# Five of the projections of a two-layer trunk by seven block products instead of eight

## The chip, the cores and the metric
One core of a Trainium2 chip runs the whole program. The metric is device time in microseconds (us) of one execution. TensorE (PE) multiplies; VectorE (DVE), ScalarE (ACT) and GpSimd (POOL) work on tiles in SBUF; SyncE (SP) issues nearly all DMAs. TensorE writes to PSUM, from which the other engines read.

## The reference
Two layers on 2048 + 256 tokens of width 1024, in float32. Layer A is attention in a window, layer B a bidirectional mLSTM; each norms its input, gates its output and adds it to x.

```python
def window_attention_mixer(xn, w_in, sink, w_out):
    proj = xn @ w_in
    q, k, v, z = jnp.split(proj, ...)          # 1024, 256, 256, 1024 columns
    ...                                        # rope, softmax over a band of keys, with a sink
    return (o * jax.nn.silu(z)) @ w_out

def mlstm_mixer(xn, w_in, gate_bias, head_norm, w_out):
    proj = xn @ w_in
    q, k, v, o, z, g = jnp.split(proj, cuts, axis=-1)   # 512, 512, 1024, 1024, 1024, 16 columns
    ...                                        # forward and backward mLSTM in chunks, summed, normed by head
    h = h * jax.nn.sigmoid(o) * jax.nn.silu(z)
    return h @ w_out

def trunk(x, ...):
    for i in range(DEPTH):
        xn = rms_norm(x, norm_g[i])
        x = x + (window_attention_mixer(xn, ...) if i % 2 == 0 else mlstm_mixer(xn, ...))
    return rms_norm(x, final_norm_g)
```

## The kernel before
The 2304 tokens are 18 tiles of 128. A product in float32 is made of three matmuls in a faster 32-bit format: `split` and `load_w` cut each operand into a rounded part "hi" (a cast, mostly on ScalarE) and a rest "lo" (a subtraction, mostly on VectorE), and `project` adds hi*hi, hi*lo and lo*hi in PSUM (L166 to L168). A projection of one tile to one block of 512 columns is 8 K tiles of 128 times these three, 24 matmuls with the activations as weights of the array (128x128) and the weight matrix as the moving 128x512 operand.

The stages follow each other: `attn_core` (q, k, v and the attention, a software pipeline of generators over the tiles), `attn_out` (z gate, times the attention's output O^T read back from DRAM, out projection, residual, norm, and the transposed xn2T written to DRAM), `mlstm_qkv` (five column blocks of a tile), `gate_sums`, `mlstm_gates_states` (the o and z gates, four blocks of a tile, and the backward states between them), `mlstm_core`. Weights lie as hi/lo slots in SBUF: 16 in the pool `w`, 8 in `wy`, 8 in `wx`, so that the blocks of the next stage can be formed while the last is still in use. Raw pieces stream through small rings (`rawx` 3, `raww` 4, split activations `xhi`/`xlo` 4).

The order within each engine is not written out by hand: a list scheduler places the instructions of the whole program by their dependences, buffers and its own estimates, and each engine then works through its own list in that order. An instruction whose input is late holds up all that stand behind it on its engine.

Of the kernel before, what the change touches and what calls it, by code (L numbers as in the profile page):

```python
# [35 lines left out]
NXB = 0  # L36
# [8 lines left out]
PH1, PL1 = (1, 5), (4,)  # L45
LASTB = (0, 1, 2, 3)
EA, ES, EQ = 2, 18, 0
ORDER = "cubwbubccucbcbuwubbbbbbw"
PHI = (1, 3, 5, 7)
PLO = (2, 6)  # L50
# [9 lines left out]
class Trunk:  # L60
    def __init__(self, nc, tc, ctx, a):
# [10 lines left out]
        # the gates of all tokens and what follows from them; layer A's staging of O^T before  # L72
# [6 lines left out]
        # reciprocal softmax sums, in the attention output's order of heads  # L79
        self.den = cp.tile([128, NT, 2, 4, 2], F32, tag="den", name="den")  # L80
        self.wp = ctx.enter_context(tc.tile_pool(name="w", bufs=16))
        self.sp = ctx.enter_context(tc.tile_pool(name="stage", bufs=1))
        self.xp = ctx.enter_context(tc.tile_pool(name="xparts", bufs=NXA))
        self.slots = lambda pool, n: [(pool, {"tag": "xhi"}, {"tag": "xlo"})] * n
        self.xring, self.nx = self.slots(self.xp, NXA), 0
# [3 lines left out]
        self.xn2T = dt("xn2T", [128, D])  # L89
# [6 lines left out]
    def stage(self, src, tag="rawx", bufs=None, pool=None):  # L96
        """A streamed [128, n] piece of DRAM."""
        n = src.shape[-1]
        raw = (pool or self.sp).tile([128, UW], F32, tag=tag, name=tag, bufs=bufs or NRX)
        self.nc.sync.dma_start(raw[:, :n], src)  # L100
        return raw[:, :n]

    def split(self, src, eng=None):
        """hi/lo float32r parts of four [128, 128] K tiles."""
        nc = self.nc
        # a ring over the pools' slots
        pool, *kw = self.xring[self.nx % len(self.xring)]
        self.nx += 1
        hi, lo = (pool.tile([128, 512], F32R, name=n, **k) for n, k in zip(("xhi", "xlo"), kw))
        nc.scalar.copy(hi[:], src)  # L110
        (eng or nc.vector).tensor_sub(lo[:], src, hi[:].bitcast(F32))  # L111
# [6 lines left out]
    def load_w(self, src, units, g=None, first=0, pool_hi=(), pool_lo=(), before={}):  # L118
        """All slabs of a weight matrix, column unit by column unit; w[block][kt] = (hi, lo, width)."""
# [3 lines left out]
        for i, widths in enumerate(units, first):  # L123
            n = sum(widths)
            pool = self.wp if i < 2 else (self.wy if i == 2 else self.wx)
            blocks = [[] for _ in widths]
            for kt in range(KT):
                if kt in before:
                    fn, *args = before[kt]
                    fn(*args)  # L130
                uw = UW if i == 3 else 512
                lo = pool.tile([128, uw], F32R, tag="wl", name="wlo")
                hi = pool.tile([128, uw], F32R, tag="wh", name="whi")
                raw = self.stage(src[kt * 128:(kt + 1) * 128, c0:c0 + n], "raww", NRW)
                gk = None if g is None else g[:, kt:kt + 1]
                if kt in pool_lo:
                    if g is not None:
                        nc.gpsimd.tensor_scalar(raw, raw, gk, 1.0, ALU.mult, ALU.mult)
                    nc.scalar.copy(hi[:, :n], raw)
                    nc.gpsimd.tensor_sub(lo[:, :n], raw, hi[:, :n].bitcast(F32))  # L140
                else:
                    if kt in pool_hi:
                        nc.gpsimd.tensor_scalar(hi[:, :n], raw, 1.0 if g is None else gk, 1.0, ALU.mult, ALU.mult)
                    elif g is None:
                        nc.scalar.copy(hi[:, :n], raw)
                    else:
                        nc.scalar.activation(hi[:, :n], raw, AF.Copy, scale=gk)  # L147
                    if g is None:
                        nc.vector.tensor_sub(lo[:, :n], raw, hi[:, :n].bitcast(F32))
                    else:  # L150
                        nc.vector.scalar_tensor_tensor(lo[:, :n], raw, gk, hi[:, :n].bitcast(F32), ALU.mult, ALU.subtract)  # L151
                c = 0
                for j, wd in enumerate(widths):
                    blocks[j].append((hi[:, c:c + wd], lo[:, c:c + wd], wd))
                    c += wd
# [3 lines left out]

    def project(self, o, xs, wb, kts=range(KT)):  # L160
        """o = x @ (one column block of w), in three float32r passes."""
# [8 lines left out]
    def rms(self, pool, src, out, n=D):  # L170
        """out[128,1] = (mean(src^2) + eps)^-1/2"""
# [11 lines left out]
    def attn_core(self):  # L183
        nc, tc, a = self.nc, self.tc, self.a
        with ExitStack() as st:
# [43 lines left out]
            def q(t, hf, xs, cs):  # L229
# [4 lines left out]
                # rotary embedding: y = x * [cos|cos] + swap(x) * [-sin|sin]  # L234
# [7 lines left out]
                # even head of a pair: [hi; lo], odd head: [lo; hi]  # L242
# [9 lines left out]
            # the first tiles' halves come between the first slabs that meet them  # L252
# [4 lines left out]

            w = self.load_w(a["w_qkv"], [[512]], self.g[:, 0], before={k: (half, t, h) for k, t, h in STARTS})
# [6 lines left out]
            w += self.load_w(a["w_qkv"][:, 512:], [[512]] * 2, self.g[:, 0], first=1)  # L265

            def core(t):
# [9 lines left out]
                def scores():  # L277
                    for g in range(KVH):
# [27 lines left out]
                        # the weights stay unnormalised; 1 / sum joins the gate  # L306
# [52 lines left out]
    def attn_out(self):  # L359
        nc, tc, a = self.nc, self.tc, self.a  # L360
        with ExitStack() as st:
            pg = st.enter_context(tc.tile_pool(name="a2g", bufs=4, reuse_waits="tile"))
            p = st.enter_context(tc.tile_pool(name="a2", bufs=2, reuse_waits="tile"))
            pt = st.enter_context(tc.tile_pool(name="a2tr", bufs=1, space=PSUM, reuse_waits="tile"))
            ps = st.enter_context(tc.tile_pool(name="a2ps", bufs=1, space=PSUM, reuse_waits="tile"))
            G = {}

            X, HG = {}, {}

            def load(t):  # L370
                X[t] = self.load_x(a["xT"][t])

            def zgate(t, b):
                pz = self.pj()
                self.project(pz, X[t], wz[b])
                rs = self.rstd[:, t:t + 1]
                gt = pg.tile([128, 512], F32, tag="G", name="G")
                nc.scalar.activation(gt[:], pz[:], AF.Sigmoid, scale=rs)
                nc.vector.scalar_tensor_tensor(gt[:], pz[:], rs, gt[:], ALU.mult, ALU.mult)
                gh = gt[:].rearrange("p (h d) -> p h d", d=HD)  # L380
                nc.gpsimd.tensor_mul(gh, gh, self.den[:, t, b].rearrange("p c g -> p (c g)").unsqueeze(2).to_broadcast([128, 8, HD]))
                G[t, b] = gt

            def gated(t):
                HG[t] = []
                for b in range(2):
                    oT = self.wg.tile([128, 512], F32, tag="oT", name="oT")
                    nc.sync.dma_start(oT[:], self.oT[t][:, b * 512:(b + 1) * 512])
                    tp = pt.tile([128, 4, 128], F32, tag="tr", name="tr")
                    for j in range(4):  # L390
                        nc.tensor.transpose(tp[:, j, :], G[t, b][:, j * 128:(j + 1) * 128], self.ident[:])
                    nc.vector.tensor_mul(oT[:], oT[:], tp[:].rearrange("p c q -> p (c q)"))
                    HG[t] += self.split(oT[:])

            def residual(t):
                x = p.tile([128, D], F32, tag="x", name="x", bufs=2)
                nc.sync.dma_start(x[:], a["x"][t * 128:(t + 1) * 128, :])
                return x

            def out(t, b, x):  # L400
                po = (ps.tile([128, 512], F32, tag="po", name="po", bufs=2) if t else self.pj())
                self.project(po, HG[t], wo[b])
                nc.vector.tensor_add(x[:, b * 512:(b + 1) * 512], x[:, b * 512:(b + 1) * 512], po[:])  # L403

            def norm(t, x):
                nc.sync.dma_start(self.x2[t][:], x[:])
                rs = p.tile([128, 1], F32, tag="rs", name="rs", bufs=2)
                self.rms(p, [x[:, :512], x[:, 512:]], rs[:])
                nc.gpsimd.tensor_scalar(x[:], x[:], rs[:], 1.0, ALU.mult, ALU.mult)
                for b in range(2):  # L410
                    tp = ps.tile([128, 4, 128], F32, tag="tr2", name="tr2", bufs=1)
                    for j in range(4):
                        nc.tensor.transpose(tp[:, j, :], x[:, (b * 4 + j) * 128:(b * 4 + j + 1) * 128], self.ident[:])
                    xo = p.tile([128, 4, 128], F32, tag="xo", name="xo", bufs=2)
                    nc.scalar.copy(xo[:], tp[:])
                    nc.sync.dma_start(self.xn2T[t][:, b * 512:(b + 1) * 512], xo[:].rearrange("p c q -> p (c q)"))

            load(0)
            load(1)
            wz = self.load_w(a["w_z"], [[512]] * 2, self.g[:, 0], 0, PHI, PLO)  # L420
            wo = self.load_w(a["w_ao"], [[512]], None, 2, PHI, PLO)
            for b in range(2):
                for t in range(2):
                    zgate(t, b)
            for t in range(NT):
                if t > 1 and t + 1 < NT:
                    load(t + 1)
# [496 lines left out]
```

## Time and profile before

| what | value |
|---|---|
| runs | 2364.59, 2367.21, 2369.46 us; median 2367.21 |
| profiled execution | span 2366.8 us, mean granted TensorE clock 0.994 |
| TensorE busy | 2323.3 us, 98% |
| VectorE / ScalarE / GpSimd busy | 1122.7 / 904.8 / 392.1 us |
| HBM read / written | 185.01 / 78.41 MB |

The times of the runs and the profiled span are those of whole executions; the profile lists no other time of its own execution than the span. Busy times of TensorE come from records that overlap. A line of the groups names the source line, the engine, the operation, the tiles out<-in, how often it runs, its busy time and mean duration, and the idle time before it with what ended it.

### The profile page before, as it was taken

Reading aid. Unit: us, or ns where it says so; the run is one execution under the profiler, and the core shown is the slowest. Engines: PE = TensorE matmul, PEld = TensorE weight load, DVE = VectorE, ACT = ScalarE, POOL = GpSimd, SP = SyncE. Lnnn points to the kernel's source line nnn. Section 1 sums busy time; section 2 is a strip of 40 time slices with the busy share of each in tenths; the row PEclk is TensorE's granted clock in tenths of the full one; section 3 lists DMA queues with packets and bytes.
Section 4 is the critical chain, followed back from the end, with each engine's and each line's share of the span. In section 5 each row is a group of like instructions: output and inputs, shape, how many; then the busy total and the mean of one; then the engine's idle time right before and its main releaser. Section 6 shows DMA issues by size and latency. Waiting matters only on the chain.

```text
span 2366.8 us, 31795 instructions
## 1 busy us (share of the span) xinstructions
PE 2323.3 (98%) x11582; PEld 1853.7 (78%) x11582; DVE 1122.7 (47%) x2731; ACT 904.8 (38%) x2149; POOL 392.1 (17%) x372
## 2 busy tenths in 40 slices
PE   8999999999999999999999999999999999999998
PEld 6767666767677888887788888888888887888887
DVE  5566656565864222225311111353333336777785
ACT  5454545454564222224211111343222236554453
POOL 3212121211321111113100000000000003333320
PEclk9999999999999999999999999999999999999999
DMA  6211111111214333335422221444323346566651
GB/s 219 65 42 47 42 47 38 52 33 43 94 63 146 119 103 116 107 116 174 139 90 82 75 85 72 147 137 151 104 89 112 104 137 214 190 223 214 211 177 67
DMA packets 129659, 265.49 MB, mean 112 GB/s; under 512 B 14272, under 2 KB 17120, under 8 KB 129504
## 3 DMA queue, kind: packets, MB, share of 16 engines
q1 hardware_dynamic: 129360, 263.46, 33.6%
q8 instruction: 91, 1.49, 0.3%
q14 instruction: 64, 0.52, 0.1%
q10 hardware_dynamic: 144, 0.01, 0.0%
HBM read 185.01 MB, written 78.41 MB: 111 GB/s over the span
## 4 chain that ended last, share of the span: by engine, by line
PE 40%; DMA 3%; DVE 3%; ACT 2%; POOL 2%; issue 1%; SPq 0%; POOLq 0%; DVEq 0%; ACTq 0%
PE pj L166 12%; PE pj L168 12%; PE pj L167 12%; DMA qs<-rows 2%; PE cu L614 1%; DVE hh L764 1%; ACT E L723 1%; POOL qs L728 1%; PE tr L457 1%; DVE xlo L111 1%; PE num L743 1%; POOL ss L757 1%; PE num L745 0%; DMA E<-rows 0%; DVE x L804 0%
## 5 line engine op out<-in xcount | busy, mean ns | idle before, releaser
L166 PE MATMUL pj<-whi,xhi 128*128 128x512 f32 (+2 forms) x2320 | 893.9, 386 | 12.7 <-ACT whi L147 5.8
L168 PE MATMUL pj<-whi,xlo 128*128 128x512 f32 (+2 forms) x2320 | 884.1, 384 | 5.1 <-DVE xlo L111 5.1
L167 PE MATMUL pj<-wlo,xhi 128*128 128x512 f32 (+2 forms) x2320 | 886.1, 382 | 0.0
L168 PEld LDWEIGHTS pj<-whi,xlo 128*128 128x128 f32 x2320 | 438.2, 189 | 100.5 <-issue 13.0
L166 PEld LDWEIGHTS pj<-whi,xhi 128*128 128x128 f32 x2320 | 438.6, 189 | 100.0 <-ACT whi L147 11.7
L167 PEld LDWEIGHTS pj<-wlo,xhi 128*128 128x128 f32 x2320 | 438.3, 189 | 81.1 <-issue 4.9
L302 ACT ACTIVATE Sm<-Sm,nm 128x384 f32<-128x384 f32 (+1 forms) x288 | 166.9, 581 | 69.4 <-DVE nm L296 69.1
L291 DVE CUSTOM_DVE_ANT_0 Sm<-s,mask 128x384 f32<-128x384 f32 (+1 forms) x272 | 137.1, 528 | 80.0 <-PE s L289 76.8
L329 PE MATMUL o<-PT,V 128*64 128x512 f32 x400 | 146.3, 620 | 4.7 <-DVE PT L319 4.7
L110 ACT CAST xhi<-rawx 128x512 fp32r<-128x512 f32 x144 | 87.4, 618 | 156.3 <-PE pj L167 100.8
L316 PEld LDWEIGHTS ptp<-ident,Sm 128*128 128x128 f32 x800 | 93.8, 141 | 62.7 <-issue 33.3
L316 PE MATMUL ptp<-ident,Sm 128*128 128x128 f32 x800 | 125.7, 278 | 2.3 <-ACT PT L319 1.6
L151 DVE SCALAR_TENSOR_TENSOR wlo<-raww,g,whi 128x512 fp32r<-128x512 f32 (+1 forms) x112 | 93.4, 857 | 50.0 <-ACT whi L147 36.6
L319 DVE COPY PT<-ptp 128x512 f32<-128x512 f32 x128 | 86.8, 686 | 62.1 <-PE ptp L316 28.6
L166 PE MATMUL po<-whi,xhi 128*128 128x512 f32 x272 | 108.2, 398 | 1.3 <-DVE x L403 1.3
L167 PE MATMUL po<-wlo,xhi 128*128 128x512 f32 x272 | 107.0, 394 | 0.0
L168 PE MATMUL po<-whi,xlo 128*128 128x512 f32 x272 | 104.3, 393 | 0.0
L176 ACT ACTIVATE junk<-x 128x512 bf16<-128x512 f32 x72 | 45.3, 630 | 151.4 <-DVE x L403 128.6
L111 DVE TENSOR_TENSOR xlo<-rawx,xhi 128x512 fp32r<-128x512 f32 x110 | 75.0, 696 | 58.3 <-ACT xhi L110 56.4
L288 PE MATMUL s<-KH,Q 128*128 128x384 f32 (+1 forms) x288 | 100.9, 362 | 0.9 <-DVE mx L291 0.8
L618 DVE SCALAR_TENSOR_TENSOR C<-C,scr,cu 128x258 f32<-128x258 f32 x112 | 52.3, 477 | 90.4 <-PE cu L614 89.4
L289 PE MATMUL s<-KL,Q 128*128 128x384 f32 (+1 forms) x288 | 92.1, 330 | 0.0
(194 smaller groups left out, 2965.1 us busy)
## 6 DMA issues: line engine op xcount, KB each, us to landing
rawx<-xT SPq DMA_DIRECT2D x72, 256.0 KB, 2.9
x<-x SPq DMA_DIRECT2D x36, 512.0 KB, 2.6
rawx<-xn2T SPq DMA_DIRECT2D x72, 256.0 KB, 3.8
rawx<-v SPq DMA_DIRECT2D x68, 258.0 KB, 3.2
go<-go SPq DMA_DIRECT2D x32, 512.0 KB, 3.6
v<-v SPq DMA_DIRECT2D x18, 516.0 KB, 3.6
rawx<-x SPq DMA_DIRECT2D x36, 256.0 KB, 2.8
oT<-scr SPq DMA_DIRECT2D x36, 256.0 KB, 2.0
```

What stands on the lines that cost most here:

```text
L110: nc.scalar.copy(hi[:], src)
L111: (eng or nc.vector).tensor_sub(lo[:], src, hi[:].bitcast(F32))
L151: nc.vector.scalar_tensor_tensor(lo[:, :n], raw, gk, hi[:, :n].bitcast(F32), ALU.mult, ALU.subtract)
L166: nc.tensor.matmul(o[:, :n], xh, wh, start=kt == 0, stop=False)
L167: nc.tensor.matmul(o[:, :n], xh, wl, start=False, stop=False)
L168: nc.tensor.matmul(o[:, :n], xl, wh, start=False, stop=kt == KT - 1)
L288: nc.tensor.matmul(S[:, :nk, :], q, KH[:, g, win, :], start=True, stop=False)
L289: nc.tensor.matmul(S[:, :nk, :], q, KL[:, g, win, :], start=False, stop=True)
L291: nc.vector.tensor_tensor_reduce(Sm[:, :nk], S[:, :nk], mask[:, t % 3, win, :], 1.0, MASKED, ALU.add, ALU.max, mx[:, c:c + 1])
L302: nc.scalar.activation(Sg[c][:, :nk], Sg[c][:, :nk], AF.Exp, bias=nm[:, c:c + 1], scale=HD ** -0.5, accum_out=rs[:, c:c + 1])
L316: nc.tensor.transpose(tp[:, c, :], Ss[g][c][:, j, :], self.ident[:])
L329: nc.tensor.matmul(o[gg * 64:(gg + 1) * 64, :], vof[sl[j]][:, g * HD:(g + 1) * HD], PTs[g][j][:], start=j == 0, stop=j == nk - 1)
```

## The change
Five projections of 1024 columns (z, out, q|k together, and o|z as two halves) are computed on pairs of tiles: the two tiles' 256 tokens by 1024 features are cut into quarters a11, a12 (first tile's halves), a21, a22 (second tile's), the weight matrix into b11 to b22 of 512x512. Seven products of sums and differences of these quarters (Winograd's form) replace eight products of quarters. `WOPS` and `XOPS` name the operands in the order of use.

```python
XOPS = ("a11", "s2", "a12", "s3", "s1", "a22", "s4")
WOPS = ("b11", "t2", "b21", "t3", "t1", "t4", "b22")

def winograd_w(self, src, c0, g=None):          # 28 hi/lo slots; L196 scales a raw piece by g
    def part(op, i, raw):
        hi, lo = self.slot()
        at[op, i] = self.taken[-1]
        nc.scalar.copy(hi[:], raw)                               # L202
        nc.vector.tensor_sub(lo[:], raw, hi[:].bitcast(F32))     # L203
        W[op][i] = hi[:], lo[:], 512
    for i in range(4):
        part("b11", i, load(i, 0, 0))
    for i in range(4):
        t1, b12, b22, b21 = load(i, 0, 0), load(i, 0, 1), load(i, 1, 1), load(i, 1, 0)
        t2 = self.raw("raww")[:, :512]
        nc.gpsimd.tensor_sub(t1, b12, t1)                        # L211
        nc.gpsimd.tensor_sub(t2, b22, t1)                        # L212
        part("t2", i, t2)
        part("b21", i, b21)
        nc.gpsimd.tensor_sub(b12, b22, b12)                      # L215
        part("t3", i, b12)
        part("t1", i, t1)
        nc.gpsimd.tensor_sub(b21, b21, t2)                       # L218
        part("t4", i, b21)
        part("b22", i, b22)

def winograd_x(self, s0, s1, X):                # seven split() (L124 cast, L125 lo) a pair
    a11 = load(s0, 0);  X["a11"] = self.split(a11);  yield
    a21, a22 = load(s1, 0), load(s1, 1)
    nc.gpsimd.tensor_add(x1, a21, a22)                           # L236
    nc.gpsimd.tensor_sub(x2, x1, a11)                            # L237
    X["s2"] = self.split(x2);  yield
    ...                                         # L243 a11 - a21 for s3, L248 a12 - x2 for s4

def half_product(self, o, xs, ws, more=False):  # 12 matmuls, L258 to L260
    ...

def winograd(self, pair, X, W, use, side):      # side(): the next step of the next pair's winograd_x
    a, b = self.pj(), self.pj()
    self.half_product(a[:], X["a11"], W["b11"])
    nc.scalar.copy(u1, a[:]);                                        side()
    self.half_product(b[:], X["s2"], W["t2"])
    nc.vector.tensor_add(u2, u1, b[:]);                              side()   # L273
    self.half_product(a[:], X["a12"], W["b21"], True)
    use(t0, 0, a[:], None);                                          side()
    self.half_product(c[:], X["s3"], W["t3"])
    nc.vector.tensor_add(u3, u2, c[:]);                              side()   # L280
    self.half_product(d[:], X["s1"], W["t1"])
    use(t1, 1, d[:], u3);                                            side()
    self.half_product(c[:], X["a22"], W["t4"], True)
    use(t1, 0, c[:], u2);                                            side()
    self.half_product(d[:], X["s4"], W["b22"], True)
    use(t0, 1, d[:], u2);                                            side()
```

`use` is what a stage does with a block: it adds u to it (in L525 for z, L559 for out, both VectorE; in L558 GpSimd adds u to x) and goes on as before (sigmoid, G at L529, times den at L531, times O^T at L537). The same diff makes these moves:

- `attn_out` is cut in two passes over all tiles: `attn_gate` writes the gated, transposed tiles to DRAM (`hgT`), and `attn_out` reads them as its activations. The residual comes in halves, and xn2T is multiplied by the row g on VectorE as it leaves PSUM, so that the weights of layer B are no longer scaled.
- `mlstm_qkv` does q|k on pairs of tiles and then v and the gates tile by tile, with xn2T read a second time; `mlstm_gates_states` does the two halves of o|z one after the other, with xn2T read for each, and one backward state after each pair. The o|z products all go to DRAM, and `mlstm_core` reads them back.
- Weights live in 31 hi/lo slots taken from one queue (16 + 8 + `NWX` 7), of which a pass uses 28; the next pass takes the three that are free and then each slot as the last pair is done with it, in the order of `WOPS`.
- The rings grow between the two cores: split activations 4 to 6, `rawx` 3 to 6, `raww` 4 to 7. Two PSUM banks (c, d) come from a pool of their own.

How the lists of the engines change is seen at three places. First TensorE, near the end of the attention core: the scores' transposes (ptp) and O = P V (o) of the last tiles, and the z projection (pj). Before:

```order
L167 MATMUL pj<-wlo,xhi 128x512
L168 MATMUL pj<-whi,xlo 128x512
L166 MATMUL pj<-whi,xhi 128x512 [waits DVE_49]
L316 MATMUL ptp<-ident,Sm 128x128 [waits Activation_49]
L316 MATMUL ptp<-ident,Sm 128x128
L316 MATMUL ptp<-ident,Sm 128x128 [waits Activation_49]
L316 MATMUL ptp<-ident,Sm 128x128
L316 MATMUL ptp<-ident,Sm 128x128 [waits Activation_49]
L316 MATMUL ptp<-ident,Sm 128x128
L167 MATMUL pj<-wlo,xhi 128x512
L316 MATMUL ptp<-ident,Sm 128x128 [waits Activation_49]
L316 MATMUL ptp<-ident,Sm 128x128
```

After, the last P V products and the start of the z pass:

```order
L484 MATMUL o<-PT,V 64x512
L484 MATMUL o<-PT,V 64x512 [waits Activation_49]
L484 MATMUL o<-PT,V 64x512
L484 MATMUL o<-PT,V 64x512 [waits DVE_49]
L258 MATMUL pj<-whi,xhi 128x512 [waits Activation_49]
L259 MATMUL pj<-wlo,xhi 128x512
L260 MATMUL pj<-whi,xlo 128x512 [waits DVE_49]
L258 MATMUL pj<-whi,xhi 128x512 [waits Activation_49]
L259 MATMUL pj<-wlo,xhi 128x512 [waits DVE_49]
L260 MATMUL pj<-whi,xlo 128x512
L258 MATMUL c<-whi,xhi 128x512 [waits PE_49,Activation_49]
L258 MATMUL d<-whi,xhi 128x512 [waits PE_49]
```

Before, the matmuls of the z projection stand between the transposes; now all but 12 of them stand behind the core, and the first ones wait for the weights' hi (ScalarE) and lo parts (VectorE).

Second, VectorE where the second weights of layer A's end are formed: wlo are the low parts of w_ao, G and oT belong to the z gate, xlo are low parts of activations. Before:

```order
L149 TENSOR_TENSOR wlo<-raww,whi 128x512 x4
L379 SCALAR_TENSOR_TENSOR G<-pj,rstd,G 128x512
L149 TENSOR_TENSOR wlo<-raww,whi 128x512
L403 TENSOR_TENSOR x<-x,pj 128x512
L149 TENSOR_TENSOR wlo<-raww,whi 128x512 x3
L111 TENSOR_TENSOR xlo<-oT,xhi 128x512 x2
L379 SCALAR_TENSOR_TENSOR G<-pj,rstd,G 128x512
L111 TENSOR_TENSOR xlo<-rawx,xhi 128x512
L403 TENSOR_TENSOR x<-x,pj 128x512
```

After, in the last pairs of the z pass:

```order
L525 TENSOR_TENSOR s<-c,u 128x512
L125 TENSOR_TENSOR xlo<-rawx,xhi 128x512
L203 TENSOR_TENSOR wlo<-raww,whi 128x512
L537 TENSOR_TENSOR oT<-oT,tr 128x512
L203 TENSOR_TENSOR wlo<-raww,whi 128x512
L529 SCALAR_TENSOR_TENSOR G<-s,rstd,G 128x512
L525 TENSOR_TENSOR s<-d,u 128x512
L203 TENSOR_TENSOR wlo<-raww,whi 128x512
L125 TENSOR_TENSOR xlo<-rawx,xhi 128x512
L203 TENSOR_TENSOR wlo<-raww,whi 128x512 x2
L529 SCALAR_TENSOR_TENSOR G<-s,rstd,G 128x512
L537 TENSOR_TENSOR oT<-oT,tr 128x512
```

Before, eight low parts (one column block) come near the start of the z gate, and the blocks are formed ahead of their stage; now all 28 of the out pass come where the z pass ends, between the low parts of activations and the gate's own work.

Third, GpSimd at the same place: L381 is G times den, L409 the norm's scaling. Before:

```order
L409 TENSOR_SCALAR x<-x,rs 128x1024
L381 TENSOR_TENSOR G<-G,den 128x512 x2
L180 TENSOR_TENSOR rs<-ss,epst 128x1
L409 TENSOR_SCALAR x<-x,rs 128x1024
L381 TENSOR_TENSOR G<-G,den 128x512 x2
L180 TENSOR_TENSOR rs<-ss,epst 128x1
```

After:

```order
L215 TENSOR_TENSOR raww<-raww 128x512
L531 TENSOR_TENSOR G<-G,den 128x512
L218 TENSOR_TENSOR raww<-raww 128x512
L211 TENSOR_TENSOR raww<-raww 128x512
L212 TENSOR_TENSOR raww<-raww 128x512
L215 TENSOR_TENSOR raww<-raww 128x512
L531 TENSOR_TENSOR G<-G,den 128x512
L218 TENSOR_TENSOR raww<-raww 128x512
L531 TENSOR_TENSOR G<-G,den 128x512
L236 TENSOR_TENSOR rawx<-rawx 128x512
L237 TENSOR_TENSOR rawx<-rawx 128x512
```

Before, GpSimd had two products with den and one scaling for each tile; now the weights' differences (raww) and the activations' sums (rawx) stand between them.

More of the change, by code (lines that the diff above doesn't have):

```diff
@@ L130, in load_w @@
                     fn(*args)
[L131 to L134, printed above, removed]
+                raw = self.stage(src[kt * 128:(kt + 1) * 128, c0:c0 + n], "raww")
                 gk = None if g is None else g[:, kt:kt + 1]
[L136 to L151, printed above, removed]
@@ L158, in load_w, with release, load @@
         return w
+    def release(self):
+        self.free.extend(self.taken)
+        self.taken = []
+    def winograd_w(self, src, c0, g=None):
+        nc = self.nc
+        W = {k: [None] * 4 for k in WOPS}
+        at = {}
+        def load(i, row, col):
+            kt = row * 4 + i
+            raw = self.stage(src[kt * 128:(kt + 1) * 128, c0 + col * 512:c0 + (col + 1) * 512], "raww")
+            if g is not None:
+                nc.scalar.mul(raw, raw, g[:, kt:kt + 1])
+            return raw
+        def part(op, i, raw):
[19 more added lines that the diff above has]
+            part("b22", i, b22)
+        self.taken = [at[op, i] for op in WOPS for i in range(4)]
+        return W
@@ new lines, in winograd_pass @@
+    def winograd_pass(self, xT, W, use, done=None, following=None, first=None):
+        X = first
+        if X is None:
+            X = {}
+            for _ in self.winograd_x(xT[0], xT[1], X):
+                pass
+        for n, pair in enumerate(PAIRS):
+            nxt = {}
+            after = (xT[pair[0] + 2], xT[pair[1] + 2]) if n + 1 < len(PAIRS) else following
+            gen = self.winograd_x(*after, nxt) if after else iter(())
+            self.winograd(pair, X, W, use, lambda: next(gen, None))
+            for _ in gen:
+                pass
+            if done:
+                done(n, pair)
+            X = nxt
+        self.release()
+        return X
@@ L405, in norm @@
[L405 to L413, printed above, removed]
+                        nc.tensor.transpose(tp[:, j, :], x[b][:, j * 128:(j + 1) * 128], self.ident[:])
@@ L806, in back @@
                 yield
+            self.free = deque(x for x in self.free if x[0] is self.wp)
             for _ in weights(0):
```

406 lines of the change are left out of this document (230 added, 176 removed).

## The prediction
> **What bounds the kernel now.** I read the page first: the totals, the slices, the costliest groups.
>
> ```profile
> span 2366.8 us, 31795 instructions
> PE 2323.3 (98%) x11582; PEld 1853.7 (78%) x11582; DVE 1122.7 (47%) x2731; ACT 904.8 (38%) x2149; POOL 392.1 (17%) x372
> PE   8999999999999999999999999999999999999998
> PEclk9999999999999999999999999999999999999999
> L166 PE MATMUL pj<-whi,xhi 128*128 128x512 f32 (+2 forms) x2320 | 893.9, 386 | 12.7 <-ACT whi L147 5.8
> L110 ACT CAST xhi<-rawx 128x512 fp32r<-128x512 f32 x144 | 87.4, 618 | 156.3 <-PE pj L167 100.8
> ```
>
> TensorE is busy in 98% of the span, in every slice, and at its full granted clock; the other engines are below half. So a matmul removed is time removed, as long as nothing else is late. Then the waits of TensorE, the few that are over a microsecond in the stages that change:
>
> ```profile
> PE pj L166 <- ACT whi L147: 5.8, 1, 5.8
> PE pj L168 <- DVE xlo L111: 5.1, 8, 1.4
> PE tr L413 <- ACT xo L415: 2.5, 1, 2.5
> PE po L166 <- DVE x L403: 1.3, 1, 1.3
> PE tr L457 <- ACT q L476: 1.2, 1, 1.2
> ```
>
> At a change of weights the old kernel loses at most a few microseconds (the 5.8 is the start of the program): its next weights lie ready in slots of their own. How much one matmul costs is not its recorded 386 ns, since records overlap. The timeline of TensorE in the q/k/v stage gives the step from start to start:
>
> ```profile
> 1299.77 0.39 PE L166 MATMUL pj<-whi,xhi 128*128 128x512 f32 x1
> ...
> 1308.01 0.40 PE L166 MATMUL pj<-whi,xhi 128*128 128x512 f32 x1
> 1308.25 0.60 PE L457 MATMUL tr<-ident,q 128*128 128x128 f32 x4
> 1308.60 0.48 PE L167 MATMUL pj<-wlo,xhi 128*128 128x512 f32 x1
> ```
>
> 36 steps lie between the first two rows: 8.24 / 36 = 0.2289 us each. Four transposes take 0.35 us (1308.25 to 1308.60).
>
> **The matmuls removed.** A projection of 18 tiles, 2 column blocks, 8 K tiles and 3 passes has 864 matmuls; 9 pairs x 7 products x 4 K tiles x 3 passes have 756. Five projections: 540 fewer, all 128x512, 540 x 0.2289 = **-123.6 us**. That holds in full only where TensorE stays the bound.
> By the Trainium skill, "TensorE: Matmul & The Clock Gate", section "Wait — 56ns, not 53.3ns?", a matmul's gap is N / 2.4 GHz + 2.5 ns, 216 ns for 512 columns, so the estimate would be 116.5 us; the trace's 229 ns decides.
>
> **What is added beside it, in a steady pair of tiles.** Prices by the rows, one instruction each:
>
> ```profile
> L111 DVE TENSOR_TENSOR xlo<-rawx,xhi 128x512 fp32r<-128x512 f32 x110 | 75.0, 696 | 58.3 <-ACT xhi L110 56.4
> L379 DVE SCALAR_TENSOR_TENSOR G<-pj,rstd,G 128x512 f32<-128x512 f32 x36 | 26.9, 746 | 4.9 <-ACT G L378 4.8
> L403 DVE TENSOR_TENSOR x<-x,po 128x512 f32<-128x512 f32 x34 | 23.3, 687 | 121.6 <-issue 64.8 <-PE po L168 56.8
> L238 POOL TENSOR_TENSOR t<-t,t 128x512 f32<-128x512 f32 x36 | 47.1, 1310 | 43.2 <-DVE t L848 21.4 <-DMA raww<-w_qkv 7.6 <-PE pj L167 6.4
> L381 POOL TENSOR_TENSOR G<-G,den 128x512 f32<-128x512 f32 x36 | 44.4, 1232 | 193.0 <-DVE G L379 190.4 <-DVE nm L296 2.6
> ```
>
> A pair costs TensorE 84 x 0.2289 = 19.2 us, with four groups of transposes 20.6. In the z pass VectorE has 7 low parts (0.70), two u and three s additions (0.69), 4 G (0.75) and 4 products with O^T (0.69): 14.1 us. GpSimd has 4 additions of halves (1.31) and 4 G times den (1.23): 10.2. ScalarE: 7 casts, u1 and 4 sigmoids at about 0.65, 7.8. The out pass by the same prices: VectorE about 12.2, GpSimd about 13 (three additions of u and four scalings more); q|k 9.7 and 5.2; o|z, with the backward states, 13.2 and 10.5. Each engine alone is hidden under 20.6, so I cost the steady part at nothing. The cover is gone only if VectorE and GpSimd run in series; that is a rival.
>
> **They do partly exclude each other.** Three pairs in the timeline:
>
> ```profile
> 1640.80 1.45 POOL L603 TENSOR_TENSOR rawx<-rawx,scr 128x512 f32<-128x512 f32 x1 [10.56 <-DVE xlo L111]
> 1641.67 1.14 DVE L670 TENSOR_TENSOR go<-go,e 128x512 f32<-128x512 f32 x1
> 1781.00 0.69 DVE L111 TENSOR_TENSOR xlo<-rawx,xhi 128x512 fp32r<-128x512 f32 x1 [0.25 <-ACT xhi L110]
> 1781.18 1.41 POOL L603 TENSOR_TENSOR rawx<-rawx,scr 128x512 f32<-128x512 f32 x1 [24.95 <-DMA rawx<-k]
> 604.13 0.68 DVE L111 TENSOR_TENSOR xlo<-rawx,xhi 128x512 fp32r<-128x512 f32 x1
> 604.36 1.59 POOL L238 TENSOR_TENSOR t<-t,t 128x512 f32<-128x512 f32 x1 [4.05 <-DVE t L848]
> ```
>
> A VectorE operation with two SBUF operands that starts under a GpSimd one ends 0.56 us after it (1642.25 to 1642.81), and the GpSimd one ends 0.90 (second pair) or 1.14 (third) after VectorE's. So of each such operation about 0.55 on VectorE and 0.90 to 1.15 on GpSimd can't overlap. In a z pair that makes ten of VectorE's x 0.55 + 4 x 1.15 + 4 x 0.90 = 13.7 us, still under 20.6.
>
> **The five changes of weights.** This is the term that counts. 28 hi/lo parts are in use in a pass and 31 slots exist, so 25 of the next 28 can be formed only as the last pair gives up its own, product by product. A change therefore puts 25 to 28 low parts on VectorE, as many casts on ScalarE, and 16 subtractions on GpSimd into the last pair and the first of the next pass, where TensorE has some 72 + 68 matmuls, 32 us. In VectorE's order from z to out the stretch from the fourth of these low parts to the last holds 25 + 10 low parts, 7 G, 6 products with O^T, 7 additions: 35 x 0.696 + 7 x 0.746 + 13 x 0.687 = 38.5 us. Its operations with two SBUF operands (39) hold 21.5 us of the exclusive share, GpSimd's (14 subtractions and 6 additions at 1.15, 7 G at 0.90) 29.3: 50.8. So TensorE is late by 38.5 - 32 = 6 at least and 50.8 - 32 = 19 at most if nothing else queues. I take the middle, **+14**. From out to q|k (35.6 and 46) and between the two o|z passes (36 and 47), bounds 4 to 19 each, as TensorE's share there is 25 to 32: **+13 and +13**. The additions of u and the low parts of the activations stand in the same in-order queue behind weight parts that wait for a slot, so TensorE then waits for L203's wlo at L259 and for L125's xlo at L260.
> From the v pass to o|z half the slots are free earlier: **+5** (0 to 10).
>
> From the attention core to z it is worse, since the order has 24 low weight parts and 7 low activation parts on VectorE after its last copy for the core and before the first u addition, 31 x 0.696 = 21.6 us; with GpSimd's subtractions, up to 36. TensorE then has 72 matmuls (16.5 us). Ahead of that the core's tail loses its filling:
>
> ```profile
> 670.00:722.00 52.00, 51.09 (x261) 34.10 (x259) 29.59 (x120) 36.86 (x100) 4.17 (x4) 1.00 0.12 41
> 670.00:722.00 52.00, 20.77 (x83) 1.00 0.12 41
> ```
>
> (From these windows on the columns are length, then busy time of PE, PEld, DVE, ACT, POOL, clock, DMA share and GB/s; the second row is TensorE's pj matmuls alone.) 83 z matmuls filled the waits of the last two tiles; the new order has 12 there. The 71 others (16.3 us) are still to be done after it: if the tail stays 52 us all of it is lost, if it shrinks to TensorE's own work nothing; 8 us. With 16 of waiting for weights (21.6 or 36 plus the last product, against 16.5) **+24**, 10 to 40.
>
> **The rest.** From o|z to the mLSTM core the last backward state is written and read back:
>
> ```profile
> Cb<-C SPq DMA_DIRECT2D x16, 516.0 KB, 3.6
> Cb<-Cb SPq DMA_DIRECT2D x16, 516.0 KB, 6.0
> ```
>
> 9.6 us at most, partly behind a product: **+4** (0 to 10). A stall also halves the granted clock for a stretch:
>
> ```profile
> 1140.00:1160.00 20.00, 17.72 (x73) 14.39 (x74) 3.61 (x6) 3.75 (x7) 0.00 (x0) 0.83 0.35 125
> 1980.00:2000.00 20.00, 15.88 (x82) 12.81 (x80) 17.78 (x39) 13.88 (x39) 10.15 (x8) 0.83 0.83 277
> ```
>
> 0.83 over 20 us is 6.8 us at half clock, 3.4 us lost. One or two of these at the new stalls, **+5** (0 to 17). The old stalls between out and q/k/v (2.5, 1.3, 1.2) with their 3.4 us of slow clock go, **-8**. The transfers: a change of weights moves 20 x 256 KB = 5.2 MB and 4 MB of tiles in some 34 us, 270 GB/s, which the second row reached (277); O^T gated makes a round trip through DRAM, but is read nine pairs later. Nothing for them.
>
> **Sum**: -123.6 + 24 + 14 + 13 + 13 + 5 + 4 + 5 - 8 = -53.6: 2366.8 becomes **2313 us**. All low ends together give 2257, all high ones 2373; the likeliest case's own range is 2275 to 2350. The profiled span of 2366.8 is 0.4 below the median of the runs (2367.2), whose spread from 2364.6 to 2369.5 makes about 0.2%, 4.7 us, what can be told from no change.
>
> **Rivals.**
> *The changes of weights are hidden.* For it speaks that slots come back one by one and nine raw buffers, with GpSimd's sums in them, can be filled ahead, so that only casts and low parts remain, 28 x 0.70 = 19.5 us over 32. Against it, VectorE's other 19 us there. Then only the core's tail costs, about 10: 2366.8 - 123.6 + 10 = **2253**. Chance 0.20.
> *The shared port paces each pair* (slower). If in the steady part the chain GpSimd sum, cast, low part, matmul, addition runs in series, a pair takes VectorE's and GpSimd's time together: z 24 us, out 25.2, o|z 23.7, against 20.6 to 21: 2.5 x 9 + 4.2 x 9 + 2.9 x 18 = 112 us. 2313 + 112 = **2425**. Against it: the parts are made a pair ahead, six buffers deep, and the exclusive share is 13.7. It decides from (53.6 + 4.7) / 36 = 1.6 us a pair on. Chance 0.12.
> *The port in full at each change.* If at the changes the exclusive sum sets the pace and whole instructions exclude each other, each of the three inner changes takes 39 x 0.696 + 20 x 1.31 + 7 x 1.23 - 32 = 30 instead of 13, and the outer two some 8 more: 2313 + 51 + 8, less the clock already counted, about **2366**, no change. Chance 0.08.
> That is the rule of the Trainium skill, "SBUF — State Buffer", section "SBUF: two separate sides": the port pair is locked for the whole instruction and the other engine fully blocks. The three timeline pairs above agree that one waits for the other, with 0.55 to 1.15 in place of the whole 0.69 to 1.31.
>
> **How the numbers follow.** My forecast 0.60, the rivals 0.20, 0.12, 0.08. Predicted is 2313. The range 2250 to 2362 leaves out the pacing rival, most of the third and the hidden case's lower third, about 0.2. Faster by over 0.2%: 0.20 + 0.57 + 0.03 = 0.80; within: 0.05; slower: 0.15, the pacing rival and the tails of the others.
>
> **What would show it.** Right: 6372 matmuls of 128x512 in place of 6912, 0.229 us apart inside a pair; five gaps of TensorE of 10 to 25 us in all each, spread over the last and first pair at a change, released by wlo or xlo on VectorE (or whi); the granted clock dips there; windows inside a pass at 20.00 of 20 us. VectorE's low parts mean above 0.70 and the z pass's first pair begins after the core's last. Wrong: gaps in every pair (the second rival), or no gaps at the changes (the first), or a step that is not 0.229, for instance because K tiles now alternate between PSUM banks.

## The result, and the profile after

The changed kernel takes 2419.2 us (median of 4 runs, 2418.5 to 2420.3), the kernel before 2367.7: ratio 1.022, 95% interval 1.0206 to 1.0235. Forecast was 2313, with 2250 to 2362 as the range. The profiled execution spans 2417.6 us, 50.8 above the 2366.8 of before.

The page of the changed kernel, the lines that answer to those shown of before:

```profile
span 2417.6 us, 32880 instructions
PE 2259.3 (93%) x11042; PEld 1776.6 (73%) x11042; DVE 1551.4 (64%) x3178; ACT 1080.3 (45%) x2476; POOL 863.5 (36%) x693
PE   8999999999968997999899999989979995999998
PEclk9999999999988998999999999989999997999999
L125 DVE TENSOR_TENSOR xlo<-rawx,xhi 128x512 fp32r<-128x512 f32 x353 | 322.8, 921 | 116.1 <-ACT xhi L124 109.0
L203 DVE TENSOR_TENSOR wlo<-raww,whi 128x512 fp32r<-128x512 f32 x140 | 161.3, 1178 | 13.5 <-ACT whi L202 12.8
```

TensorE has 540 instructions fewer, and holes where the weights change (the 6 to 8 of its row) and where the mLSTM core begins (the 5), with a lower clock in most of these slices. The mean granted clock of the execution fell from 0.994 to 0.966. The low parts take 0.92 (activations) and 1.18 us (weights) on VectorE, where the forecast priced both at 0.70; the old kernel's own weight parts (L149) took 0.83. TensorE's longest waits:

```profile
PE pj L259 <- DVE wlo L203: 15.9, 7, 3.8
PE s L835 <- DVE E L845: 13.8, 1, 13.8
PE cu L749 <- ACT vh L728: 13.6, 16, 4.3
PE pj L258 <- ACT xhi L124: 11.3, 4, 6.7
PE pj L258 <- DVE u L273: 9.2, 2, 5.3
```

Windows by stage (length, then busy PE, PEld, DVE, ACT, POOL, clock, DMA share, GB/s): the change from the attention core to z; the change from z to out; a steady pair of the out pass; the change from v to o|z; the o|z pair in which the gate sums run; a later o|z pair; the start of the mLSTM core.

```profile
702.30:755.50 53.20, 31.37 (x73) 19.41 (x74) 44.21 (x41) 31.99 (x54) 36.48 (x24) 0.62 0.52 166
926.00:971.00 45.00, 30.21 (x107) 21.72 (x107) 41.81 (x40) 16.62 (x29) 34.19 (x23) 0.77 0.57 186
970.00:991.00 21.00, 21.00 (x102) 17.43 (x101) 10.88 (x20) 5.30 (x13) 14.05 (x14) 1.00 0.53 169
1549.00:1584.00 35.00, 29.52 (x129) 22.44 (x128) 33.89 (x44) 20.76 (x34) 21.59 (x14) 0.85 0.57 181
1604.00:1640.00 36.00, 27.41 (x106) 20.98 (x106) 19.72 (x30) 20.51 (x34) 18.99 (x13) 0.81 0.31 99
1683.00:1707.00 24.00, 21.92 (x96) 16.54 (x94) 13.65 (x20) 8.17 (x15) 10.80 (x8) 1.00 0.37 115
2005.00:2030.00 25.00, 4.38 (x17) 3.79 (x18) 19.31 (x21) 16.33 (x32) 15.17 (x12) 0.57 0.96 343
```

The steady pair is full: 21.0 us. In the three changes VectorE is the busiest engine, 44.2 of 53.2, 41.8 of 45 and 33.9 of 35 us, so in the last two it is the bound. The granted clock is down to 0.62 and 0.77 in the first two. In the last row TensorE does next to nothing for 25 us.

Where the time went, from the starts of the pairs in TensorE's timeline. A pair without loss is 21.0 us in the z and out passes, 20.65 in o|z (84 x 0.2289, and 12 matmuls of a state at 0.118); the change from the attention core is counted against its time before, less 83 z matmuls; for the mLSTM core, the time from the last projection matmul of o|z to the end is 412.9 us, and was 387.7.

| place | measured loss, us | forecast | its bounds |
|---|---|---|---|
| core to z | 31 | 24 | 10 to 40 |
| z to out | 25 | 14 | 6 to 19 |
| out to q\|k | 19 | 13 | 4 to 19 |
| v to o\|z | 14 | 5 | 0 to 10 |
| first to second o\|z | 27 | 13 | 4 to 19 |
| steady pairs of z, out, q\|k | 0 | 0 | |
| the 15 other o\|z pairs | 42 | 0 | |
| into the mLSTM core | 25 | 4 | 0 to 10 |
| slow clock | in the rows above | 5 | 0 to 17 |

Together 183, with slow clock included. Less the 8 of old stalls, a figure of the forecast that was not measured by itself, that is 175; the two spans ask for 174.4, since -123.6 + 174.4 = +50.8.

### The profile page after: what moved, and what is told of

Same layout as the page of the kernel before. It is cut to its first block, busy times and chain, and to the rows that moved or that the text cites. A ratio compares the mean times of both kernels' runs of the same rounds, so it can differ in the third digit from the quotient of the medians.

```text
span 2417.6 us, 32880 instructions
## 1 busy us (share of the span) xinstructions
PE 2259.3 (93%) x11042; PEld 1776.6 (73%) x11042; DVE 1551.4 (64%) x3178; ACT 1080.3 (45%) x2476; POOL 863.5 (36%) x693
## 5 line engine op out<-in xcount | busy, mean ns | idle before, releaser
L319 PE MATMUL pj<-whi,xhi 128*128 128x512 f32 (+2 forms) x1152 | 429.4, 374 | 11.1 <-ACT whi L169 5.7
L320 PE MATMUL pj<-wlo,xhi 128*128 128x512 f32 (+2 forms) x1152 | 426.6, 370 | 0.0
L321 PE MATMUL pj<-whi,xlo 128*128 128x512 f32 (+2 forms) x1152 | 421.8, 371 | 3.7 <-DVE xlo L125 3.6
L125 DVE TENSOR_TENSOR xlo<-rawx,xhi 128x512 fp32r<-128x512 f32 x353 | 322.8, 921 | 116.1 <-ACT xhi L124 109.0
L321 PEld LDWEIGHTS pj<-whi,xlo 128*128 128x128 f32 x1152 | 217.8, 189 | 44.4 <-DVE xlo L125 7.2
L258 PE MATMUL pj<-whi,xhi 128*128 128x512 f32 x540 | 223.0, 414 | 29.3 <-ACT xhi L124 11.3
L320 PEld LDWEIGHTS pj<-wlo,xhi 128*128 128x128 f32 x1152 | 218.3, 189 | 38.1 <-issue 6.5
L259 PE MATMUL pj<-wlo,xhi 128*128 128x512 f32 x540 | 221.1, 410 | 16.1 <-DVE wlo L203 15.9
L260 PE MATMUL pj<-whi,xlo 128*128 128x512 f32 x540 | 218.4, 405 | 2.4 <-DVE xlo L125 2.3
L203 DVE TENSOR_TENSOR wlo<-raww,whi 128x512 fp32r<-128x512 f32 x140 | 161.3, 1178 | 13.5 <-ACT whi L202 12.8
```

Of the source, the lines that this page charges most:

```text
L203: nc.vector.tensor_sub(lo[:], raw, hi[:].bitcast(F32))
L258: nc.tensor.matmul(o, xh, wh, start=i == 0 and not more, stop=False, skip_group_check=more)
L259: nc.tensor.matmul(o, xh, wl, start=False, stop=False, skip_group_check=more)
L260: nc.tensor.matmul(o, xl, wh, start=False, stop=i == 3, skip_group_check=more)
L319: nc.tensor.matmul(o[:, :n], xh, wh, start=kt == 0, stop=False)
L320: nc.tensor.matmul(o[:, :n], xh, wl, start=False, stop=False)
```

## The experiments

In the table at the end of this section each time stands beside its ratio to the kernel before, taken on the same chip. All start from the changed kernel unless said. The scheduler orders each program anew, so an edit can also move instructions that it does not name. The code is cut to the lines that matter.

**The sums of weights: what do they cost, and how?** Three edits of GpSimd's four subtractions in `winograd_w`: left out; done into a buffer that nobody reads; done by VectorE.

```diff
 e1: -nc.gpsimd.tensor_sub(t1, b12, t1)   (and L212, L215, L218); part("t2", i, b22), part("t3", i, b12), ...
 e5: +nc.gpsimd.tensor_sub(dead(), b12, t1)   (and three more), parts as in e1
 e6: +nc.vector.tensor_sub(t1, b12, t1)   (and three more), parts as in the changed kernel
```

> Leaves out the 80 GpSimd subtractions that form the sums of weights (the parts are made of the raw pieces), so the outputs are not the reference's; loads, casts, low parts and matmuls stay. Theory A (shared port: at a change of weights GpSimd's subtractions and VectorE's low parts shut each other out): the mean of the low parts of weights falls from 1.18 us to under 0.85, the stretches at the five changes (now 31, 25, 19, 14 and 27 us over two pairs' work) shrink by half or more, and the time falls by 50 us or more, to about 2365. Rival B (the 28 low parts and casts with only three free slots are enough to stop TensorE): the stretches shrink by a few us each, the time stays above 2395.

> GpSimd does as many subtractions on the raw weights as in the changed kernel, into a buffer that nobody reads, and the parts are made of the raw pieces (the outputs are not the reference's). Theory A (the port: GpSimd's subtractions hold up VectorE while they run): the low parts of weights stay near 1.18 us and the time stays near the changed kernel's, 2405 to 2420. Rival G (lateness: it is the chain of load, GpSimd, cast, low part that is too long, not the port): the time falls to that of the kernel without the subtractions, about 2350.

> The sums of weights are formed by VectorE in place of GpSimd. VectorE gets 16 x 0.69 = 11 us more at each change and loses the exclusion, which by the low parts' mean (1.18 against 0.70) was 28 x 0.48 = 13 us. Theory A (port): about even, 2395 to 2425. Rival G (lateness of the GpSimd chain): faster by 40 us or more, 2380 or less.

The low parts of weights in the groups of e1, e5 and e6, in this order:

```profile
L203 DVE TENSOR_TENSOR wlo<-raww,whi 128x512 fp32r<-128x512 f32 x140 | 109.8, 817 | 9.8 <-ACT whi L202 9.5
```

```profile
L203 DVE TENSOR_TENSOR wlo<-raww,whi 128x512 fp32r<-128x512 f32 x140 | 147.9, 1089 | 7.2 <-ACT whi L202 7.1
```

```profile
L203 DVE TENSOR_TENSOR wlo<-raww,whi 128x512 fp32r<-128x512 f32 x140 | 113.2, 836 | 2.9 <-ACT whi L202 2.9
```

The totals of the same three, in the same order:

```profile
PE 2226.5 (95%) x11042; PEld 1760.3 (75%) x11042; DVE 1481.1 (63%) x3178; ACT 1078.5 (46%) x2476; POOL 737.4 (31%) x613
PE 2252.8 (94%) x11042; PEld 1773.9 (74%) x11042; DVE 1542.9 (64%) x3178; ACT 1078.7 (45%) x2476; POOL 862.4 (36%) x693
PE 2254.3 (94%) x11042; PEld 1773.2 (74%) x11042; DVE 1535.6 (64%) x3258; ACT 1080.0 (45%) x2476; POOL 744.9 (31%) x613
```

Without the subtractions the kernel takes 2350.1 us, 69 less; the five changes then lose some 41 us, not 116. With as many subtractions whose result nobody waits for it takes 2414.6: nearly all is back, 64.5 us for 80 subtractions. That alone does not rule out lateness (rival G), since these subtractions still hold raw buffers and a place in GpSimd's queue. VectorE's busy time does: with the same 3178 instructions it is 61.8 us longer in e5 than in e1. With the subtractions on VectorE (e6) it has 80 instructions more than in the changed kernel, and is busy 15.8 us less (1535.6 against 1551.4). The kernel then takes 2399.2, 20 us less than with them on GpSimd and 49 more than without them. So GpSimd holds up VectorE, theory A. Some of the 64.5 us can be slow clock that follows from the stalls (granted 0.982 in e1, 0.970 in e5), which no run separates. The timeline of the changed kernel shows the single case, at the change between the o|z passes:

```profile
1767.32 1.30 POOL L794 TENSOR_TENSOR e<-e 128x512 f32<-128x512 f32 x1 [0.74 <-ACT e L787]
1767.44 1.72 DVE L203 TENSOR_TENSOR wlo<-raww,whi 128x512 fp32r<-128x512 f32 x1
...
1774.17 0.68 DVE L125 TENSOR_TENSOR xlo<-rawx,xhi 128x512 fp32r<-128x512 f32 x1
1774.33 1.64 POOL L212 TENSOR_TENSOR raww<-raww 128x512 f32<-128x512 f32 x1 [0.63 <-DVE wlo L203]
1774.77 1.75 DVE L729 TENSOR_TENSOR v<-rawx,vh 128x516 fp32r<-128x516 f32 x1
```

A low part of weights issued under a GpSimd operation is 1.72 us long and ends 0.54 after it (1768.62 to 1769.16); the low part of activations at 1774.17 came first and took 0.68.

**The o|z pairs.**

```diff
 e2: -kw = self.weighted_k(p, t, 1)
     +kw = self.weighted_k(p, t, 1, ("raww",))          # and parts(p, self.v[t], "v", 1, ("raww",))
 e4: -W = self.winograd_w(a["w_oz"], b * 1024); X = self.winograd_pass(...)
     +w = self.load_w(a["w_oz"], [[512]] * 4)           # tile by tile, four blocks of project()
```

> The backward states' loads (k and v) use the seven raw buffers of the weights, idle inside a pass, in place of the six of the activations. Theory C (in the o|z passes the state's pieces are loaded late because they queue for the activations' buffers, and TensorE waits for them): the o|z pairs with a state go from 22 to 25 us to about 21, the time falls by about 25 us, to 2394. Rival D (those pairs are long because VectorE and GpSimd shut each other out): no change, 2415 to 2424.

> The o|z projection is done tile by tile in four column blocks with eight products of quarters' worth of matmuls, as in the kernel before; z, out and q|k stay on pairs with seven products. 216 matmuls come back, 49 us. If the o|z passes lose 84 us to late states, to the gate sums and to two changes of weights, as the trace reads, the time falls by about 35 us, to 2385 or below; if their loss is of the pairs as such, or lies elsewhere, it rises to 2440 or more.

e2 takes 2374.7 us, 45 less, more than theory C asked. The 15 o|z pairs outside the change lose 4 us and not 42, and the pair with the gate sums is 22.5 long, not 35.8. A steady pair of e2, and the waits of TensorE in its o|z pairs from 1582 to 1732:

```profile
1690.00:1711.00 21.00, 21.00 (x100) 17.53 (x99) 15.12 (x23) 10.24 (x18) 10.92 (x8) 1.00 0.48 164
```

```profile
PE c L258 <- DVE u L280: 2.0, 3, 1.0
PE pl L693 <- ACT spr L691: 0.2, 1, 0.2
```

VectorE is busier than in the changed kernel (15.1 of 21 against 13.7 of 24) and GpSimd as busy, and TensorE doesn't wait: rival D falls. The place in the changed kernel: the transfer of a piece of v is issued only as a buffer of the activations comes free (the first line is SyncE's own wait at L115 for the low parts of the activations, from 1640 to 1755), and the state's product stands in TensorE's queue behind it.

```profile
SPq L115 <- DVE xlo L125: 33.8, 14, 5.4
1693.05 0.41 SPq L115 DMA_DIRECT2D rawx<-v  x1
1697.32 0.62 ACT L728 CAST vh<-rawx 128x516 fp32r<-128x516 f32 x1 [4.01 <-DMA rawx<-v]
1697.99 0.51 PE L749 MATMUL cu<-vh,kh 128*128 128x258 f32 x2 [0.93 <-ACT vh L728]
```

e4, with 216 matmuls (49 us) put back, is 30 us faster than the changed kernel, at 2389.6: in these two passes the seven products, as the changed kernel has them, cost more than they saved. With e2's buffers they are ahead of e4 (2374.7).

**The late start of the mLSTM core.** From the end of the last pair to the core's first product of v and E (num, L864) 20.9 us pass (2004.65 to 2025.53). Before, there was no pause: 1979.07 and 1978.90. Ahead of it come only the eight scores of another tile (L835), at 2018.47, after the 13.8 us of waiting for E shown above. I moved what might hold the core up: the mask (e3); the mask, the parts of E and the rows qs together (e7); w_mo's parts (e9); v's first tile (e12); and e15 leaves out 15 of w_mo's 16 loads.

```diff
 e3:  -cm = py.tile(...)                    +cm = pe.tile(...)
 e7:  -El = p.tile(, Eh = py.tile(          +El = pn.tile(, Eh = pn.tile(    # a new pool, first on the left
 e9:  -KX, WL = 0, 0                        +KX, WL = 0, 9
 e12: pools b2 and b2s exchanged, b3v ahead of b3m
 e15: -raw = self.stage(w_mo, ...)          +raw = one
```

> The causal mask of the mLSTM core lies in a buffer that is free before the o|z passes end. Theory E (the core begins about 24 us late because the mask's load, and with it the first tile's weights E, waits for buffers that the passes hold to the end): the first product of the core comes 8 us or more earlier, the time falls to about 2408. Rival F (the other first buffers of the core are held just as long): the time stays within 5 us of 2419.

> Mask, E's hi and lo parts and the first rows of the mLSTM core lie where the o|z stage's small buffers were, in place of where weights of its last pair lie. Theory F (these buffers, held to the end of the last pair, make the core begin about 20 us late): the first product of the core comes 10 to 20 us earlier and the time falls to 2400 to 2410. Rival (VectorE and ScalarE are busy with w_mo's parts and the last pair at that time, buffers or not): within 5 us of 2419.

> The changed kernel with w_mo's 16 parts formed some steps into the first tile of the mLSTM core, in place of ahead of it (nothing else moved). Theory H (the core begins late because VectorE and ScalarE work through w_mo's parts, which get their slots only as the last pair ends, ahead of the first tile's E): the first product of the core comes 8 us or more earlier and the time falls to 2405 to 2413. Rival (the last pair's own work and the loads of E, v and k set it): 2415 or more.

> The changed kernel with the o|z stage's two pools exchanged, so that the first tile of v of the mLSTM core no longer lies where the gate tiles e and s of the last pair lie, which are read until their last write to DRAM (issued 11 us after the last matmul). Theory I (the core's first product waits for v, and v for those tiles): the first product comes about 8 us earlier, 2408 to 2414. Rival (VectorE's and ScalarE's own queue at that time sets it): 2416 or more.

> The changed kernel with one raw piece of w_mo loaded and all 16 parts made from it (the outputs are not the reference's): 15 loads of 256 KB, 3.9 MB, are left out at the start of the mLSTM core; the casts and low parts stay. Theory J (the core's start is bound by transfers: some 10 MB in 30 us at 310 to 400 GB/s, since all its loads wait for the last pair's buffers and then come at once): the products begin 5 us or more earlier and the time falls by 6 to 11 us, to 2408 to 2413. Rival (queues of VectorE, ScalarE and GpSimd): within 4 us of 2419.

None of the five made the kernel faster by more than its interval; e7 and e9 are 9 and 8 us slower, for reasons that stay open. The first product of v and E came at 2016.4 in e12 (15 us after the last pair) and at 2022.9 in e15 (18 us after), and what follows it was late all the same. The windows of the changed kernel and of e15, from 2005 to 2015 and 2015 to 2025:

```profile
2005.00:2015.00 10.00, 0.00 (x0) 0.00 (x0) 7.10 (x8) 6.84 (x10) 4.83 (x4) 0.67 0.92 316
2015.00:2025.00 10.00, 2.08 (x8) 1.78 (x8) 7.21 (x10) 7.96 (x21) 5.62 (x5) 0.50 1.04 397
```

```profile
2005.00:2015.00 10.00, 0.00 (x0) 0.00 (x0) 7.22 (x10) 9.19 (x16) 6.48 (x5) 0.72 1.02 354
2015.00:2025.00 10.00, 4.19 (x17) 3.80 (x18) 8.69 (x12) 5.76 (x14) 3.28 (x3) 0.50 0.88 299
```

The DMA engines are full or nearly so in both (0.88 to 1.04), with VectorE and ScalarE busy 58 to 92% as well. That alone makes no hole, for the old kernel's core began with as full a stretch, in which TensorE was busy 6.68 of 10 us:

```profile
1982.50:1992.50 10.00, 6.68 (x40) 4.90 (x38) 9.35 (x21) 9.97 (x29) 3.74 (x3) 0.98 1.04 374
```

Its first tile's parts were ready by then, formed under the matmuls of the last two tiles. Shown is that none of these moves, made alone, shortens the late start. That all of it counts together, because it starts only when the last pair gives its memory back, is argued and stays open; so is e15's rival, the queues of VectorE, ScalarE and GpSimd, which fits its time.

**A version without the losses found.** e8 forms the sums of weights in the attention core, keeps them in DRAM, loads 28 pieces at a change and takes slots in the order of use; the state's loads are as in e2.

```diff
+    def prepare(self):                     # one step a tile in attn_core
+        t1, b12, b22, b21 = load(0, 0), load(0, 1), load(1, 1), load(1, 0)
+        ...                                # four nc.gpsimd.tensor_sub, in place
+        nc.sync.dma_start(D_[op, i][:], x)
     def part(op, i):
+        raw = load(i, *at_[op]) if op in at_ else self.stage(self.wd[name, c0][op, i][:], "raww")
```

> The sums of weights of all five passes are formed during the attention core by GpSimd and kept in DRAM; a change of weights loads 28 pieces and forms only the hi and lo parts, in the order of use; the state's loads use the weights' raw buffers. By theory A (nothing of GpSimd for weights at a change) the stretches shrink as where the subtractions were left out (69 us), and with the state's ring (45 us) the sum is about 2310, less what the attention core loses to 80 more subtractions (0 to 20). If the loads (7.3 MB at a change) are then late, 2340 or more.

2321.0 us: faster than both, ratio 0.9805 (0.9788 to 0.9822) to the kernel before. By the spans it is 47 us below the kernel before, where the matmuls removed are worth 123.6, so some 76 us of loss are left. The first lines of its page:

```profile
span 2319.7 us, 33318 instructions
PE 2218.1 (96%) x11042; PEld 1763.5 (76%) x11042; DVE 1501.9 (65%) x3178; ACT 1085.8 (47%) x2486; POOL 840.4 (36%) x693
```

On it the core's start was tried again: w_mo later and the core's buffers on the left (e10), w_mo later alone (e11), v's tile (e14).

> Sums of weights ahead and the state's ring as in the version of 2321 us, with w_mo's parts later and the core's first buffers on the left as before. If both hold the core up together, neither alone showing it: 2300 to 2312. If neither does: 2318 to 2328.

> The version of 2321 us with w_mo's parts later alone. Theory H: 2308 to 2315. Otherwise 2318 to 2326.

> The same exchange in the version of 2321 us. Theory I: 2309 to 2316. Rival: 2318 to 2325.

2322.0, 2320.7 and 2324.8: no difference clear of noise.

| kernel | median, us | ratio to before, 95% interval |
|---|---|---|
| changed | 2419.2 | 1.022 (1.0206 to 1.0235) |
| e1 no sums of weights | 2350.1 | 0.9935 (0.992 to 0.9951) |
| e2 state's own buffers | 2374.7 | 1.0039 (1.0024 to 1.0054) |
| e3 mask early | 2418.2 | 1.022 (1.0202 to 1.0237) |
| e4 o\|z by tiles | 2389.6 | 1.0101 (1.0086 to 1.0116) |
| e5 sums unread | 2414.6 | 1.0202 (1.0184 to 1.022) |
| e6 sums on VectorE | 2399.2 | 1.0136 (1.0116 to 1.0156) |
| e7 core's E on the left | 2427.9 | 1.0259 (1.0231 to 1.0287) |
| e9 w_mo later | 2427.2 | 1.0259 (1.0235 to 1.0283) |
| e12 v's tile | 2417.3 | 1.0212 (1.0194 to 1.023) |
| e15 one w_mo piece | 2418.6 | 1.0208 (1.0188 to 1.0227) |
| e8 sums ahead, state's buffers | 2321.0 | 0.9805 (0.9788 to 0.9822) |
| e10 w_mo later, core on the left, from e8 | 2322.0 | 0.9813 (0.9795 to 0.9831) |
| e11 w_mo later, from e8 | 2320.7 | 0.9809 (0.9789 to 0.9829) |
| e14 v's tile, from e8 | 2324.8 | 0.9821 (0.9805 to 0.9837) |

## Why the prediction was wrong

- *The matmuls removed, -123.6.* Right: 540 fewer, 0.228 us from start to start inside a pair, and z, out and q|k pairs of 21.0 us without a hole, VectorE and GpSimd hidden under them as costed.
- *The changes of weights.* The mechanism was right, the size wrong: 116 us measured for 69 forecast. The mis-sized choice is "the middle" between VectorE alone (6) and the exclusive sum (19): the losses stand at or above the upper end (25, 19, 27, and 14 over a bound of 10). e1, e5 and e6 show why: VectorE is the bound there, and each of the 80 subtractions adds 61.8 / 80 = 0.77 us to its work. Weight parts were also priced too low, at 0.70 where the old kernel's took 0.83. The third rival, to which I gave 0.08, had 30 us for each of the inner changes: 25 and 27 are nearer to it than to my 14 and 13, and 19 is nearer to mine, so the pace lies between the partial and the whole exclusion. By the rule of the Trainium skill, "SBUF — State Buffer", section "SBUF: two separate sides", the second engine is blocked for the whole instruction; the 0.77 us for each subtraction agrees that GpSimd's work is time lost to VectorE, though not with the whole 1.6 us that a subtraction takes in e5.
- *Core to z, +24.* 31 us lie within its bounds, but in part by luck. The tail, to which 8 went, lost nothing: its last O product ends at 702.3 us, 20.9 earlier than before, with 16.3 us of z matmuls taken out. All the loss came behind it: the 72 matmuls left of the first pair, which with its four groups of transposes need 17.9 us, took 53.2. That is some 35 us late, where the working had 22 as the most (36 + 2.7 - 16.5).
- *The slow clock, +5.* Too small. By the forecast's own reckoning, length times the missing share of the clock, it is 14 us before (0.994 over 2366.8) and 82 after (0.966 over 2417.6). The stretch from 702.3 to 755.5 alone has 20 (0.62 over 53.2). Part of it falls where TensorE was waiting anyway, so the 68 between them can't be set beside the losses above; how much of them is slow clock stays open.
- *The steady part at nothing.* Wrong for o|z, 42 us, of which 15 are in the pair with the gate sums. The step counted engine time (13.2 and 10.5 under 20.6) and left out the transfers of the state's k and v, that share six buffers with the activations of the next pair. e2 gives 38 of the 42 back. The second rival, VectorE and GpSimd in series, ended at 2425, near the measured time, but for another reason: no z, out or q|k pair is long, and e2's pairs are full with VectorE busier.
- *Into the core, +4.* Wrong, 25. The term priced one state's round trip. What the old order had and the new has not is the overlap of the core's loads and parts with the last two tiles; that this is the whole cause is not shown.
- *The old stalls, -8.* Not measured by itself; with it the losses add up to within 1 us of the spans.
- *Slips in the working.* The middle of 6 and 19 is 12.5, not 14. All low ends together give 2259 and all high ones 2369, not 2257 and 2373. The second rival's z pair is 3 to 3.7 us longer, not 2.5, which puts that rival at 2430 to 2436. None of these decides anything here.

## What to carry to other kernels

Where a fast path adds work to GpSimd and VectorE, charge VectorE with a part of every GpSimd operation on SBUF wherever VectorE is near full (here 0.77 us of 1.6), and at the place where the operands change, not on the average. Look there for the slow clock that a stall brings, too. Count buffers by who queues for them: a small consumer that shares a ring with a big one waits for the big one's turn, and an in-order engine passes that wait to everybody. Work that depends on no late data, such as sums of weights, belongs in a stage with slack, even at the price of more transfers.

## What was not expected of the hardware

With the same 3178 instructions VectorE was busy 61.8 us longer when GpSimd made 80 subtractions that nobody reads (e5 against e1), and the kernel took 64.5 us longer. The granted clock was 0.62 over the 53.2 us of the first change, and 0.50 from 2015 to 2025 at the mLSTM core's start. The DMA engines moved 397 GB/s there; the 277 of the forecast was a mean over 20 us, and the old kernel reached 374 over 10.
